# 49 instead of 32 pairs of a down projection in seven block products, and the block sums of the input kept in DRAM

## The chip, the cores and the metric

The kernel runs on one core of one Trainium2 chip. The time is device microseconds of one execution; the kernel before took 2128.32 us (median of 3 runs, 2127.16 to 2129.32). TensorE (PE) does the matrix products, VectorE (DVE) and ScalarE (ACT) the elementwise work, GpSimd (POOL) little, and the queues of SyncE (SP) and POOL issue the transfers.

## The reference

Two encoder layers over 256 tokens of width 2048: an attention sub-layer each, and then the sub-layer that the change touches, a multilayer perceptron with 8192 hidden features:

```python
D_MODEL = 2048; SEQ = 256; DEPTH = 2; D_FF = 4 * D_MODEL
for i in range(DEPTH):
    ...                                   # attention: x = x + heads @ w_out[i]
    h = rms_norm(x, norm_mlp[i])
    x = x + jnp.square(jax.nn.relu(h @ w_up[i])) @ w_down[i]
return x
```

All inputs and outputs are float32.

## The kernel before

**Exactness by splitting.** Every float32 operand of a product is split in two (`split`, L240): `hi`, a copy in the matmul's narrower type that ACT makes (L241), and `lo`, what is left, a subtraction on DVE (L242). A product of two such operands is three matmuls (hi by hi, hi by lo, lo by hi), the function `three` (L710) in the down projection.

**Weights.** A weight arrives in pieces of 128 x 1024 (512 KB), in the order of `plan`. `fetch` (L204) issues the transfer to a `raw` tile on the SP queue (L217) and splits it to `hi` and `lo`. There are four buffers each of `raw`, `hi` and `lo`; a new transfer waits until the work that read the old contents of its buffer is done, and `fetch` runs up to two pieces ahead of the piece in use (`AHEAD`).

**Up projection.** `mlp` (L680) makes 16 chunks of 512 hidden features (`chunk_out`, L318), each from 8 weight pieces, in four PSUM banks; the tags `mm` and `aux` alternate between chunks. Behind each chunk ACT and DVE add the two halves of a bank and square the positive part (L690 to L692), into a tile `ht` of [128, 4, 256]. The hidden activations stay in SBUF.

**Down projection.** It is done in two halves of 1024 output features (`half_`). In each, the 8192 hidden features are 32 pairs `j` of 2 x 128 features. A pair takes two weight pieces, and its hidden values split to `x2` (`h2_of`, L699). It is a block product of 2 x 2 blocks: two blocks of tokens (`t`), two of outputs (`n`), two of features (`kk`). An ordinary pair makes all eight block products, three matmuls each: 24 matmuls of 128 x 512.

A pair in `FAST` goes by seven block products (`seven`, L722; Winograd's form of Strassen's scheme): 21 matmuls, for sums and differences of blocks in place of the eighth product. On the weight side `fetch_sums` (L189) makes them on DVE from the pair's two raw pieces: two sums `a` (one instruction, L194, which reads both pieces), then `b` in two steps (L196, L197); `a` and `b` are split to `ah, al, bh, bl` of the tag `x2` (8 buffers). On the input side, three DVE instructions (L729, L731, L732) make block sums of the hidden values and a split makes the tile `t2` of them, tag `h2` (6 buffers, which `x2` of `h2_of` shares). Four of the seven products go to four side banks, which `add_side` adds to the result behind the last pair of `FAST`. In the second half of the first layer the tiles of the next layer's input take four of the eight `x2` buffers, and `a` and `b` are of the tag `blk` there.

**Order of the work.** The program is written with a queue of small tasks (`Task`, `tick`, `flush`) that are put between the pieces; a scheduler of the tile framework then sets the order on each engine when the program is built. On the chip each engine works through its list in that order, and waits at an instruction until what it needs is there.

Of the kernel before, what the change touches and what calls it, by code (L numbers as in the profile page):

```python
# [22 lines left out]
P = 128  # L23
# [9 lines left out]
WAIT = 2  # L33
AHEAD = 2
WARM = 16
FAST = (5, 8, 11, 14, 17, 20, 23, 26)
LAM_INIT = 0.8 - 0.6 * math.exp(-0.3 * 0)

G_ATTN, G_MEM, G_MLP = 0, 2 * KT, 4 * KT
# [8 lines left out]
def trunk(ctx: ExitStack, tc: tile.TileContext, xin, xtok, memin, pos, rel, gcol, rows,  # L48
# [12 lines left out]
    def nm(s):  # L61
        uid[0] += 1
        return f"{s}{uid[0]}"
# [4 lines left out]
    def quad(tag, shape=(P, 2, 2, 256), dt=F32R):  # L68
        return xp.tile(list(shape), dt, tag=tag, name=nm(tag), bufs={"x2": 8, "h2": 6, "blk": 10}[tag])
# [101 lines left out]
    def plan_chunks(name, chunks):  # L171
        plan.extend((name, c, j) for c in chunks for j in range(8))

    def plan_down(name):
        plan.extend((name, h, j) for h in range(2) for j in range(64))

# [27 lines left out]
    def fetch(parts=1, lead=None):  # L204

        name, c, j = plan.popleft()
        src = weights[name][c, j]
        raw = wp.tile([P, 1024], F32, tag="raw", name=nm("raw"))
        hi = wp.tile([P, 1024], F32R, tag="hi", name=nm("hi"))
        lo = wp.tile([P, 1024], F32R, tag="lo", name=nm("lo"))  # L210
        n = 1024 // parts
        seven = name.startswith("down") and j % 2 == 1 and j // 2 in FAST
        for i in range(parts):
            s = slice(i * n, (i + 1) * n)
            if lead is not None:
                lead(i)
            behind[0] = nc.sync.dma_start(raw[:, s], src[:, s])  # L217
# [22 lines left out]
    def split(hi, lo, src):  # L240
        nc.scalar.copy(hi, src)  # L241
        nc.vector.tensor_tensor(lo, src, as32(hi), op=ALU.subtract)  # L242
# [436 lines left out]

    def mlp(layer, X2, last):  # L680
        hT = []
        wide = big([P, 6, 4, S])
        for c in range(16):
            ps = chunk_out(f"up{layer}", c, 8, lambda k: X2[k], "mm" if c % 2 == 0 else "aux", 2 if c == 0 else 1)
            if c == 0:
                mlp_stats()
            ht = wide[:, c - 4] if 4 <= c < 10 else blk([P, 4, S], F32)
            for o in range(4):
                t = t1k()
                nc.scalar.copy(t, ps[o][:, 256:512])  # L690
                nc.vector.tensor_tensor(t, ps[o][:, 0:256], t, op=ALU.add)
                nc.vector.scalar_tensor_tensor(ht[:, o, :], t, 0.0, t, op0=ALU.max, op1=ALU.mult)  # L692
            hT.append(ht)
        N2 = Halves()

        def hidden(j):
            return hT[j // 2].rearrange("p k s -> p (k s)")[:, (j % 2) * 512:(j % 2) * 512 + 512]

        def h2_of(j):  # L699
            t = quad("h2", (P, 2, 512))  # L700
            split(t[:, 0, :], t[:, 1, :], hidden(j))
            return t


        for half_ in range(2):
            tag = "mm" if half_ == 0 else "aux"
            ps = [[bank(tag) for _ in range(2)] for _ in range(2)]
            chunks = (2 * half_, 2 * half_ + 1)

            def three(bank_, first_, last_, x2, xs, w2, ws):  # L710
                nc.tensor.matmul(bank_, lhsT=x2[:, 0, xs], rhs=w2[0][:, ws], start=first_, stop=False)  # L711
                nc.tensor.matmul(bank_, lhsT=x2[:, 0, xs], rhs=w2[1][:, ws], start=False, stop=False)  # L712
                nc.tensor.matmul(bank_, lhsT=x2[:, 1, xs], rhs=w2[0][:, ws], start=False, stop=last_)  # L713

            lower, upper = slice(0, 512), slice(512, 1024)

            def mms(n, t, k, two, x2):
                w2 = two[(k + n) % 2]
                three(ps[n][t], k == 0, k == 4 * KT - 1, x2, slice((k % 2) * S + t * P, (k % 2) * S + (t + 1) * P), w2,
                      upper if n else lower)  # L720

            def seven(j, two, x2):  # L722

                ah, al, bh, bl = [v.rearrange("p a n -> p (a n)") for v in sums.pop((f"down{layer}", half_, 2 * j + 1))]
                t2 = quad("h2", (P, 2, 512))
                v = t2k([P, 512])
                h = hidden(j)
                h4 = h.rearrange("p (a s) -> p a s", a=4)
                nc.vector.tensor_tensor(v[:, 0:256].rearrange("p (a s) -> p a s", a=2), h4[:, 0:4:3, :],  # L729
                                        h4[:, 1:2, :].broadcast_to([P, 2, P]), op=ALU.subtract)  # L730
                nc.vector.tensor_tensor(v[:, 256:384], h[:, 384:512], v[:, 0:128], op=ALU.add)  # L731
                nc.vector.tensor_tensor(v[:, 384:512], h[:, 256:384], v[:, 256:384], op=ALU.subtract)  # L732
                split(t2[:, 0, :], t2[:, 1, :], v)
                at = [slice(i * P, (i + 1) * P) for i in range(4)]
                f, e = j == FAST[0], j == FAST[-1]
                three(side[0], f, e, x2, at[0], two[0], lower)
                three(ps[0][0], False, False, x2, at[2], two[1], lower)
                three(ps[1][0], False, False, t2, at[3], two[0], upper)
                three(side[1], f, e, t2, at[0], (ah, al), upper)
                three(side[3], f, e, t2, at[1], (ah, al), lower)  # L740
                three(side[2], f, e, t2, at[2], (bh, bl), lower)
                three(ps[0][1], False, False, x2, at[3], (bh, bl), upper)

            def add_to(n, t, src):
                c = chunks[n]
                d = xt[:, t, c * 512:(c + 1) * 512]
                nc.vector.scalar_tensor_tensor(d, src, r2[:, t:t + 1], d, op0=ALU.mult, op1=ALU.add)
                return c, d

            def add_side():  # L750

                q1, u2, u3, u4, u5 = [t2k([P, 512]) for _ in range(5)]
                nc.scalar.copy(q1, side[0])
                nc.vector.tensor_tensor(u2, side[2], q1, op=ALU.subtract)
                nc.vector.tensor_tensor(u4, side[1], u2, op=ALU.subtract)
                nc.vector.tensor_tensor(u3, u2, side[3], op=ALU.subtract)
                nc.vector.tensor_tensor(u5, u3, side[1], op=ALU.subtract)
                add_to(0, 0, q1)
                add_to(0, 1, u4)
                add_to(1, 0, u3)  # L760
                add_to(1, 1, u5)

            def finish(n, t):
                c, d = add_to(n, t, ps[n][t])
                if last:
                    nc.sync.dma_start(out[:, t * D + c * 512:t * D + (c + 1) * 512], d)

            held = []
            for j in range(32):
                if j == FAST[0]:  # L770
# [6 lines left out]
                if j in FAST:  # L777
# [6 lines left out]
                if j == FAST[-1]:  # L784
# [12 lines left out]
        return N2  # L797

# [147 lines left out]
```

## Time and profile before

| what | us |
|---|---|
| median of 3 runs | 2128.32 |
| the profiled execution | 2127.94 |
| its span, first to last instruction | 2126.1 |
| first layer: up projection (427.8 to 785.3 of the span) | 357.5 |
| first layer: down projection, first half (785.3 to 954.0) | 168.7 |
| first layer: down projection, second half (954.0 to 1122.6) | 168.6 |
| second layer: down projection, begins at | 1784 |

The span is the time between the first and the last instruction; the execution's own time is 1.8 us longer. The granted clock of TensorE was 0.999. In the views below "busy" counts the time in which an engine worked on something, x the instructions, and a time in square brackets is how long the engine had been idle before a row, with what ended the idle time.

### The profile page before, as it was taken

What the parts mean: (1) busy time and instruction counts of PE and PEld (TensorE: products, weight loads), DVE (VectorE), ACT (ScalarE), POOL (GpSimd) and SP (SyncE); (2) the same over time, 40 slices, a digit from 0 to 9 for tenths busy, and PEclk for the clock granted to TensorE, in tenths of its full rate; (3) what the DMA queues carried; (4) which work ended last, traced back from release to release, by engine and by line L of the source; (5) the groups of instructions that cost most, each with busy time, mean ns of one, the idle gap of its engine ahead of it and who ended that gap; (6) DMA issues with size and microseconds to landing.
All of it is one profiled execution on the core that took longest, in us unless ns stands there. A gap on an engine that the chain in (4) does not pass through costs nothing.

```text
span 2126.1 us, 29324 instructions
## 1 busy us (share of the span) xinstructions
PE 2116.4 (100%) x11020; PEld 1790.6 (84%) x11020; DVE 1497.5 (70%) x2259; ACT 1130.8 (53%) x1712; POOL 34.3 (2%) x61
## 2 busy tenths in 40 slices
PE   9999999999999999999999999999999999999999
PEld 7878878888888888888888888888888888888887
DVE  7667786566565558889886677655555556888896
ACT  6456675454444446656655566554444444665564
POOL 1200020000000000000000000000000000000000
PEclk9999999999999999999999999999999999999999
DMA  8864564666666655555766556466666666566654
GB/s 292 238 211 150 159 194 154 186 180 190 191 184 196 188 190 200 197 198 198 250 205 191 178 167 187 149 180 188 188 189 190 186 192 193 190 215 210 203 193 158
DMA packets 114958, 409.23 MB, mean 192 GB/s; under 512 B 13568, under 2 KB 14336, under 8 KB 114560
## 3 DMA queue, kind: packets, MB, share of 16 engines
q1 hardware_dynamic: 111840, 401.01, 59.7%
q0 software_dynamic: 1536, 4.20, 0.8%
q10 hardware_dynamic: 1440, 2.15, 0.3%
q8 instruction: 86, 1.41, 0.3%
q14 instruction: 56, 0.46, 0.1%
HBM read 401.93 MB, written 5.37 MB: 192 GB/s over the span
## 4 chain that ended last, share of the span: by engine, by line
PE 97%; DMA 1%; DVE 1%; ACT 1%; issue 0%; SPq 0%; POOL 0%; ACTq 0%; DVEq 0%; POOLq 0%
PE mm L325 11%; PE aux L325 11%; PE mm L312 9%; PE mm L314 9%; PE mm L313 9%; PE mm L329 6%; PE aux L329 6%; PE aux L711 5%; PE aux L712 5%; PE mm L711 5%; PE mm L712 5%; PE aux L713 5%; PE mm L713 5%; PE aux L404 1%; DMA raw<-in_w_a 1%; PE aux L375 1%
## 5 line engine op out<-in xcount | busy, mean ns | idle before, releaser
L242 DVE TENSOR_TENSOR lo<-raw,hi 128x1024 fp32r<-128x1024 f32 (+1 forms) x744 | 875.4, 1190 | 535.3 <-ACT hi L241 534.0
L241 ACT CAST hi<-raw 128x1024 fp32r<-128x1024 f32 (+1 forms) x744 | 751.7, 1024 | 760.9 <-PE aux L325 193.5
L312 PE MATMUL mm<-hi,x 128*128 128x512 f32 x704 | 281.5, 401 | 0.7 <-ACT hi L241 0.7
L313 PE MATMUL mm<-lo,x 128*128 128x512 f32 x704 | 276.8, 393 | 2.6 <-DVE lo L242 2.6
L314 PE MATMUL mm<-hi,x 128*128 128x512 f32 x704 | 276.5, 393 | 0.0
L325 PE MATMUL mm<-x,hi 128*128 128x512 f32 x1024 | 247.4, 391 | 0.0
L325 PE MATMUL aux<-x,hi 128*128 128x512 f32 x1024 | 246.9, 391 | 0.0
L325 PEld LDWEIGHTS mm<-x,hi 128*128 128x128 f32 x1024 | 188.2, 188 | 36.8 <-DVE xt L675 0.5
L325 PEld LDWEIGHTS aux<-x,hi 128*128 128x128 f32 x1024 | 188.2, 188 | 36.4
L712 PE MATMUL aux<-lo,h 128*128 128x512 f32 x432 | 168.2, 389 | 0.0
L713 PE MATMUL aux<-hi,h 128*128 128x512 f32 x432 | 168.1, 389 | 0.0
L711 PE MATMUL aux<-hi,h 128*128 128x512 f32 x432 | 168.1, 389 | 0.0
L711 PE MATMUL mm<-hi,h 128*128 128x512 f32 x432 | 168.0, 389 | 0.0
L712 PE MATMUL mm<-lo,h 128*128 128x512 f32 x432 | 168.0, 389 | 0.0
L713 PE MATMUL mm<-hi,h 128*128 128x512 f32 x432 | 168.0, 389 | 0.0
L313 PEld LDWEIGHTS mm<-lo,x 128*128 128x128 f32 x704 | 133.1, 189 | 28.4 <-DVE lo L242 4.2
L314 PEld LDWEIGHTS mm<-hi,x 128*128 128x128 f32 x704 | 132.6, 188 | 28.0
L312 PEld LDWEIGHTS mm<-hi,x 128*128 128x128 f32 x704 | 132.6, 189 | 27.2 <-ACT hi L241 1.3
L329 PEld LDWEIGHTS mm<-x,lo 128*128 128x128 f32 x1024 | 131.4, 191 | 4.8
L329 PEld LDWEIGHTS aux<-x,lo 128*128 128x128 f32 x1024 | 131.3, 191 | 5.0
L329 PE MATMUL mm<-x,lo 128*128 128x256 f32 x1024 | 133.3, 283 | 0.0
L329 PE MATMUL aux<-x,lo 128*128 128x256 f32 x1024 | 132.8, 283 | 0.0
(207 smaller groups left out, 2526.0 us busy)
## 6 DMA issues: line engine op xcount, KB each, us to landing
raw<-in_w_up SPq DMA_DIRECT2D x256, 512.0 KB, 3.8
raw<-in_w_down SPq DMA_DIRECT2D x256, 512.0 KB, 4.3
raw<-in_w_a SPq DMA_DIRECT2D x72, 512.0 KB, 4.0
raw<-in_w_out SPq DMA_DIRECT2D x64, 512.0 KB, 3.6
raw<-in_w_b SPq DMA_DIRECT2D x48, 512.0 KB, 3.7
raw<-in_w_mem SPq DMA_DIRECT2D x32, 512.0 KB, 4.0
raw<-in_w_a SPq DMA_DIRECT2D x16, 256.0 KB, 5.2
blk<-bkt POOLq DMA_DIRECT2D x32, 128.0 KB, 8.6
```

The costliest lines, as they stand in the source:

```text
L241: nc.scalar.copy(hi, src)
L242: nc.vector.tensor_tensor(lo, src, as32(hi), op=ALU.subtract)
L312: nc.tensor.matmul(ps[t], lhsT=xh, rhs=hi[:, ws], start=(k == 0), stop=False)
L313: nc.tensor.matmul(ps[t], lhsT=xh, rhs=lo[:, ws], start=False, stop=False)
L314: nc.tensor.matmul(ps[t], lhsT=xl, rhs=hi[:, ws], start=False, stop=(k == KT - 1))
L325: nc.tensor.matmul(ps[o], lhsT=hi[:, cols(k % 2, o)], rhs=x2.rearrange("p a s -> p (a s)"), start=(k == 0), stop=(k == 2 * nj - 1))
L329: nc.tensor.matmul(ps[o][:, 256:512], lhsT=lo[:, cols(k % 2, o)], rhs=x2[:, 0, :], start=False, stop=False)
L375: nc.tensor.transpose(out=pt[:, h * P:(h + 1) * P], in_=qn[t][:, h * P:(h + 1) * P], identity=ident)
L404: nc.tensor.transpose(out=pt[:, kt * S + qt * P:kt * S + (qt + 1) * P], in_=p_of(qt)[:, kt * P:(kt + 1) * P], identity=ident)
L711: nc.tensor.matmul(bank_, lhsT=x2[:, 0, xs], rhs=w2[0][:, ws], start=first_, stop=False)
L712: nc.tensor.matmul(bank_, lhsT=x2[:, 0, xs], rhs=w2[1][:, ws], start=False, stop=False)
L713: nc.tensor.matmul(bank_, lhsT=x2[:, 1, xs], rhs=w2[0][:, ws], start=False, stop=last_)
```

## The change

`FAST` becomes every second pair from 3 to 27 (13 pairs instead of 8), and every second pair from 9 to 27 (`LATE`, 10 pairs) in the second half of the first layer: 13 + 10 + 13 + 13 = 49 pairs instead of 4 x 8 = 32. The block sums of the hidden values are no longer made in the down projection. A task `keep_sums` for each such pair is put behind its chunk of the up projection: the three DVE instructions, the split to a tile of tag `h2`, and a transfer of the tile (512 KB) to DRAM on the POOL queue. In the down projection `seven` reads that tile back by a transfer on the POOL queue, once in each half.

```diff
-FAST = (5, 8, 11, 14, 17, 20, 23, 26)
+FAST = tuple(range(3, 28, 2))
+LATE = tuple(range(9, 28, 2))
...
+    def fast_pairs(name, h):
+        return LATE if (name, h) == ("down0", 1) else FAST
...
-        seven = name.startswith("down") and j % 2 == 1 and j // 2 in FAST
+        seven = name.startswith("down") and j % 2 == 1 and j // 2 in fast_pairs(name, c)
...
+        def keep_sums(j):
+
+            t2 = quad("h2", (P, 2, 512))
+            v = t2k([P, 512])
+            h = hidden(j)
+            h4 = h.rearrange("p (a s) -> p a s", a=4)
+            nc.vector.tensor_tensor(v[:, 0:256].rearrange("p (a s) -> p a s", a=2), h4[:, 0:4:3, :],
+                                    h4[:, 1:2, :].broadcast_to([P, 2, P]), op=ALU.subtract)
+            nc.vector.tensor_tensor(v[:, 256:384], h[:, 384:512], v[:, 0:128], op=ALU.add)
+            nc.vector.tensor_tensor(v[:, 384:512], h[:, 256:384], v[:, 256:384], op=ALU.subtract)
+            split(t2[:, 0, :], t2[:, 1, :], v)
+            kept[j] = dp.tile([P, 2, 512], F32R, name=nm("kept"))
+            nc.gpsimd.dma_start(kept[j], t2)
...
             hT.append(ht)
+            for j in (2 * c, 2 * c + 1):
+                if any(j in fast_pairs(f"down{layer}", h) for h in range(2)):
+                    Task([lambda j=j: keep_sums(j)], wait=2)
...
+        flush()
...
             def seven(j, two, x2):
...
-                v = t2k([P, 512])
-                h = hidden(j)
-                h4 = h.rearrange("p (a s) -> p a s", a=4)
-                nc.vector.tensor_tensor(v[:, 0:256].rearrange("p (a s) -> p a s", a=2), h4[:, 0:4:3, :],
-                                        h4[:, 1:2, :].broadcast_to([P, 2, P]), op=ALU.subtract)
-                nc.vector.tensor_tensor(v[:, 256:384], h[:, 384:512], v[:, 0:128], op=ALU.add)
-                nc.vector.tensor_tensor(v[:, 384:512], h[:, 256:384], v[:, 256:384], op=ALU.subtract)
-                split(t2[:, 0, :], t2[:, 1, :], v)
+                nc.gpsimd.dma_start(t2, kept[j])
```

The other lines of the diff put `fast[0]` and `fast[-1]` where `FAST[0]` and `FAST[-1]` stood.

The scheduler's order on DVE in the middle of the first layer's first half, before: one ordinary pair, one ordinary pair, and a pair by seven products. `lo` are splits of weight pieces, `h2` splits of hidden values (from `t2k`: of the block sums), L194 makes the sums `a`, L196 and L197 the two steps of `b`, and `x2` are the splits of `a` and `b`.

```order
L242 TENSOR_TENSOR lo1605_8438<-raw1603_8436,hi1604_8437 128x1024
L242 TENSOR_TENSOR lo1608_8444<-raw1606_8442,hi1607_8443 128x1024
L242 TENSOR_TENSOR h21638_8582<-big930_4604,h21638_8582 128x512
L242 TENSOR_TENSOR h21651_8634<-big930_4604,h21651_8634 128x512
L194 TENSOR_TENSOR x21616_8485<-raw1610_8475,raw1613_8481 128x1024
L196 TENSOR_TENSOR x21617_8486<-x21616_8485,raw1610_8475 128x512
L197 TENSOR_TENSOR x21617_8486<-x21617_8486,raw1613_8481 128x512
L242 TENSOR_TENSOR x21619_8493<-x21616_8485,x21618_8492 128x1024
L242 TENSOR_TENSOR x21621_8495<-x21617_8486,x21620_8494 128x1024
L242 TENSOR_TENSOR lo1612_8477<-raw1610_8475,hi1611_8476 128x1024
L242 TENSOR_TENSOR lo1615_8483<-raw1613_8481,hi1614_8482 128x512
L242 TENSOR_TENSOR h21658_8673<-blk1288_6773,h21658_8673 128x512
```

The same engine at the same place, with the change: first an ordinary pair (raw1574 and raw1577) and the pair by seven products behind it (raw1582 and raw1585). Lines have moved: L246 is the split, L198 makes `a`, L200 and L201 make `b`.

```order
L246 TENSOR_TENSOR lo1576_8212<-raw1574_8210,hi1575_8211 128x1024
L246 TENSOR_TENSOR lo1579_8218<-raw1577_8216,hi1578_8217 128x1024
L198 TENSOR_TENSOR x21588_8258<-raw1582_8248,raw1585_8254 128x1024
L246 TENSOR_TENSOR lo1584_8250<-raw1582_8248,hi1583_8249 128x1024
L200 TENSOR_TENSOR x21589_8259<-x21588_8258,raw1582_8248 128x512
L246 TENSOR_TENSOR lo1587_8256<-raw1585_8254,hi1586_8255 128x512
L201 TENSOR_TENSOR x21589_8259<-x21589_8259,raw1585_8254 128x512
L246 TENSOR_TENSOR x21591_8266<-x21588_8258,x21590_8265 128x1024
L246 TENSOR_TENSOR h21615_8363<-big930_4604,h21615_8363 128x512
L246 TENSOR_TENSOR x21593_8268<-x21589_8259,x21592_8267 128x1024
L246 TENSOR_TENSOR h21622_8402<-big930_4604,h21622_8402 128x512
```

And right behind it the next ordinary pair (raw1595 and raw1598) and the next pair by seven products (raw1603 and raw1606):

```order
L198 TENSOR_TENSOR x21609_8348<-raw1603_8338,raw1606_8344 128x1024
L246 TENSOR_TENSOR lo1597_8302<-raw1595_8300,hi1596_8301 128x1024
L246 TENSOR_TENSOR lo1600_8308<-raw1598_8306,hi1599_8307 128x1024
L246 TENSOR_TENSOR lo1605_8340<-raw1603_8338,hi1604_8339 128x1024
L200 TENSOR_TENSOR x21610_8349<-x21609_8348,raw1603_8338 128x512
L246 TENSOR_TENSOR lo1608_8346<-raw1606_8344,hi1607_8345 128x512
L201 TENSOR_TENSOR x21610_8349<-x21610_8349,raw1606_8344 128x512
L246 TENSOR_TENSOR x21612_8356<-x21609_8348,x21611_8355 128x1024
L246 TENSOR_TENSOR h21636_8453<-big930_4604,h21636_8453 128x512
L246 TENSOR_TENSOR x21614_8358<-x21610_8349,x21613_8357 128x1024
L246 TENSOR_TENSOR h21643_8492<-big930_4604,h21643_8492 128x512
```

Before, `a` stood behind the splits of both ordinary pairs that precede its pair. Now it stands behind the splits of the one ordinary pair in every second case, and ahead of them in the others: the two forms alternate, six times the second form in each half with 13 such pairs, twice in the half with 10.

On DVE in the up projection, behind the work of a chunk (L713 and L714 were L691 and L692), the block sums (L697, L699, L700) and their split stand between the splits of the next chunk's weights:

```order
L714 SCALAR_TENSOR_TENSOR blk1351_7060<-t1k1354_7069 128x256
L714 SCALAR_TENSOR_TENSOR blk1351_7060<-t1k1355_7073 128x256
L246 TENSOR_TENSOR lo1365_7089<-raw1363_7087,hi1364_7088 128x1024
L697 TENSOR_TENSOR t2k1367_7126<-blk1351_7060 128x256
L246 TENSOR_TENSOR lo1371_7136<-raw1369_7134,hi1370_7135 128x1024
L699 TENSOR_TENSOR t2k1367_7126<-blk1351_7060,t2k1367_7126 128x128
L700 TENSOR_TENSOR t2k1367_7126<-blk1351_7060,t2k1367_7126 128x128
L246 TENSOR_TENSOR lo1374_7142<-raw1372_7140,hi1373_7141 128x1024
L246 TENSOR_TENSOR h21366_7125<-t2k1367_7126,h21366_7125 128x512
L246 TENSOR_TENSOR lo1377_7180<-raw1375_7178,hi1376_7179 128x1024
```

Before, at the other chunks' ends the same place held only the splits of weights, apart from a few block sums of early pairs that the scheduler had put there already.

More of the change, by code (lines that the diff above doesn't have):

```diff
@@ L681, in mlp, with hidden @@
         hT = []
+        kept = {}
         wide = big([P, 6, 4, S])
+        def hidden(j):
+            return hT[j // 2].rearrange("p k s -> p (k s)")[:, (j % 2) * 512:(j % 2) * 512 + 512]
+        def keep_sums(j):
[10 more added lines that the diff above has]
+            nc.gpsimd.dma_start(kept[j], t2)
         for c in range(16):
@@ L693, in mlp @@
             hT.append(ht)
+            for j in (2 * c, 2 * c + 1):
+                if any(j in fast_pairs(f"down{layer}", h) for h in range(2)):
+                    Task([lambda j=j: keep_sums(j)], wait=2)
         N2 = Halves()
-        def hidden(j):
-            return hT[j // 2].rearrange("p k s -> p (k s)")[:, (j % 2) * 512:(j % 2) * 512 + 512]
         def h2_of(j):
@@ L708, in mlp @@
             chunks = (2 * half_, 2 * half_ + 1)
+            fast = fast_pairs(f"down{layer}", half_)
             def three(bank_, first_, last_, x2, xs, w2, ws):
@@ L725, in seven @@
                 t2 = quad("h2", (P, 2, 512))
[L726 to L733 removed]
+                nc.gpsimd.dma_start(t2, kept[j])
                 at = [slice(i * P, (i + 1) * P) for i in range(4)]
[L735 removed]
+                f, e = j == fast[0], j == fast[-1]
                 three(side[0], f, e, x2, at[0], two[0], lower)
@@ L769, in mlp @@
             for j in range(32):
-                if j == FAST[0]:
+                if j == fast[0]:
                     side = [bank("aux" if half_ == 0 else "mm") for _ in range(4)]
@@ L776, in mlp @@
                     continue
-                if j in FAST:
+                if j in fast:
                     seven(j, two, x2)
@@ L783, in mlp @@
                                 mms(n, t, 2 * j + kk, two, x2)
-                if j == FAST[-1]:
+                if j == fast[-1]:
                     add_side()
```

## The prediction

> **What bounds the kernel now.** I read the page first: busy time by engine, and the chain of work that ended last.
>
> ```profile
> span 2126.1 us, 29324 instructions
> PE 2116.4 (100%) x11020; PEld 1790.6 (84%) x11020; DVE 1497.5 (70%) x2259; ACT 1130.8 (53%) x1712; POOL 34.3 (2%) x61
> PE 97%; DMA 1%; DVE 1%; ACT 1%; issue 0%; SPq 0%; POOL 0%; ACTq 0%; DVEq 0%; POOLq 0%
> ```
>
> PE is on 97% of the chain. But a busy PE can be a slow PE, so I took the rate next, from the timeline of PE in a down projection, nine matmuls apart (818.20 to 819.79 stand between):
>
> ```profile
> 817.97 0.39 PE L711 MATMUL mm<-hi,h 128*128 128x512 f32 x1
> ...
> 820.01 0.39 PE L711 MATMUL mm<-hi,h 128*128 128x512 f32 x1
> ```
>
> One starts every 2.04 / 9 = 0.2267 us. An ordinary pair is 24 x 0.2267 = 5.44 us, one by seven products 21 x 0.2267 = 4.76 us. A half of the first layer's down projection has 24 of the one and 8 of the other: 168.6 us. The windows by stage (the first row is the up projection, the others the two halves) show just that, so PE doesn't stall there at all:
>
> ```profile
> core 0: us, PE busy (x) PEld busy (x) DVE busy (x) ACT busy (x) POOL busy (x), PEclk, DMA share, GB/s
> 427.80:785.30 357.50, 357.50 (x2058) 315.84 (x2057) 206.73 (x282) 158.05 (x204) 0.00 (x0) 1.00 0.61 189
> 785.30:954.00 168.70, 168.70 (x746) 139.71 (x745) 143.45 (x168) 99.05 (x125) 0.00 (x0) 1.00 0.58 198
> 954.00:1122.60 168.60, 168.60 (x754) 139.82 (x752) 146.79 (x182) 100.76 (x130) 3.50 (x2) 1.00 0.63 215
> ```
>
> DVE is busy 85% of the first half (143.45 of 168.70): the engine to watch when work moves from PE to DVE. The clock is 1.00 and cancels.
>
> **What the change takes away.** 17 more pairs by seven products, three matmuls less each: 51 x 0.2267 = 11.56 us of PE's time, if PE stays the bound.
>
> **What DVE has to do for it.** The timeline of DVE in the first half, one pair by seven products and the ordinary pair behind it:
>
> ```profile
> 850.05 1.29 DVE L242 TENSOR_TENSOR h<-big,h 128x512 fp32r<-128x512 f32 x2
> 851.34 1.23 DVE L194 TENSOR_TENSOR x<-raw,raw 128x1024 f32<-128x1024 f32 x1
> 852.60 0.69 DVE L196 TENSOR_TENSOR x<-x,raw 128x512 f32<-128x512 f32 x1
> 853.32 0.69 DVE L197 TENSOR_TENSOR x<-x,raw 128x512 f32<-128x512 f32 x1
> 853.93 2.42 DVE L242 TENSOR_TENSOR x<-x,x 128x1024 fp32r<-128x1024 f32 x2
> 856.27 1.82 DVE L242 TENSOR_TENSOR lo<-raw,hi 128x1024 fp32r<-128x1024 f32 x2
> 858.01 0.69 DVE L242 TENSOR_TENSOR h<-big,h 128x512 fp32r<-128x512 f32 x1
> 860.10 2.36 DVE L242 TENSOR_TENSOR lo<-raw,hi 128x1024 fp32r<-128x1024 f32 x2 [1.41 <-ACT hi L241]
> 862.38 0.69 DVE L242 TENSOR_TENSOR h<-t2k,h 128x512 fp32r<-128x512 f32 x1
> ```
>
> Ends overlap the next start, so I count from start to start: two splits of 1024 take 862.38 - 860.10 = 2.28, 1.14 each; the pair at 856.27 (one of 1024, one of 512) takes 1.74, so 0.60 for 512. A pair by seven products without its block sums is `a`, one `lo` and two splits of sums (4 x 1.14), the two steps of `b`, the short `lo` and one hidden split (4 x 0.60): 6.96 us. An ordinary pair is 2 x 1.14 + 0.60 = 2.88. With the change the two alternate: DVE needs 9.84 us where PE needs 5.44 + 4.76 = 10.20. It fits with 0.36 to spare. The block sums would not have fitted:
>
> ```profile
> L729 DVE TENSOR_TENSOR t2k<-big 128x256 f32<-128x256 f32 x16 | 6.6, 421 | 0.0
> L731 DVE TENSOR_TENSOR t2k<-big,t2k 128x128 f32<-128x128 f32 x16 | 4.4, 286 | 0.0
> L732 DVE TENSOR_TENSOR t2k<-big,t2k 128x128 f32<-128x128 f32 x16 | 4.5, 289 | 0.3
> ```
>
> These and a split of 512 take about 1.4 us, overlaps taken off: 11.2 a round.
>
> **Where the sums go.** 26 of them (13 a layer) stand in the up projections, 1.4 us of DVE and a cast of 0.6 on ACT each. DVE is busy there 206.73 of 357.50 us, and the timeline behind a chunk shows that a delay of that size is already borne: two hidden splits between the weights' splits, and then it waits for ACT, which waits for PE.
>
> ```profile
> 457.55 0.69 DVE L242 TENSOR_TENSOR h<-blk,h 128x512 fp32r<-128x512 f32 x1
> 458.23 1.23 DVE L242 TENSOR_TENSOR lo<-raw,hi 128x1024 fp32r<-128x1024 f32 x1
> 461.98 1.23 DVE L242 TENSOR_TENSOR lo<-raw,hi 128x1024 fp32r<-128x1024 f32 x1 [2.53 <-ACT hi L241]
> ```
>
> I cost them at nothing, hidden by PE's 22 us a chunk. If that cover were gone, 26 x 1.4 = 36 us. The stores and loads on POOL's queue block nobody behind them: POOL has no other work there but two selects on the bias table, and tag `h2` has six buffers of which a round takes three, so each load may start when PE is done with the pair four back, 15 us before its tile is needed.
>
> **The loop that I expect to bind.** The 0.36 us of spare time counts only while DVE never waits. A weight's transfer waits for its buffer, by SP's waits in the first half:
>
> ```profile
> SPq L217 <- DVE lo L242: 140.6, 63, 8.2
> ```
>
> With four `raw` buffers and two pairs of two pieces in turn, the pieces of one pair by seven products always take the buffers of the one before. The last reader of its second piece is the second step of `b`. So from there to the next `a` lies at least a transfer, D:
>
> ```profile
> raw<-in_w_down SPq DMA_DIRECT2D x256, 512.0 KB, 4.3
> L217 SPq DMA_DIRECT2D raw<-in_w_down x4: 327/328/328, 845.7 to 850.2; - x4
> DMA to landing us min/median/max: 3.7/4.4/4.5
> ...
> L217 SPq DMA_DIRECT2D raw<-in_w_down x4: 327/328/328, 1064.4 to 1067.8; - x4
> DMA to landing us min/median/max: 3.8/5.1/5.9
> ```
>
> Issued four in 4.5 us, the slowest takes 4.5 us; four in 3.4 us, 5.9. Where `a` stands behind the ordinary pair's splits, DVE has 3.48 (two splits of sums, two hidden) + 2.28 = 5.76 us of other work in the meantime. Where the scheduler put `a` ahead of them (every second time), it has 3.48 only, and stands still with those two splits, ready to go, queued behind `a`; PE waits for them.
>
> Worked out, with times from PE's start of a pair by seven products: the ordinary pair's casts on ACT need `hi` buffers that PE frees 0.68 us before and at that start, 2.00 us for both,
>
> ```profile
> 859.01 2.00 ACT L241 CAST hi<-raw 128x1024 fp32r<-128x1024 f32 x2 [1.93 <-issue]
> ```
>
> so its second `lo` ends at 2.8, and `a`, `lo`, step, short `lo`, step end at 2.8 + 1.14 + 1.14 + 0.60 + 0.60 + 0.69 = 7.0. In the next round `a` starts at 7.0 + D, and the second `lo` ends 3.51 later: at D + 0.31 after that round's start (10.20). PE reads it 4.76 + 4 x 0.2267 = 5.67 after it. From then on two rounds take DVE D + 6.45 (`a` to the last step) + 9.84 = D + 16.29 against PE's 20.40: it falls D - 4.11 further behind each time.
>
> D lies between 4.5 and 5.9; one below 4.2 would make the loop harmless. The changed kernel moves five 512 KB transfers in 10.2 us where four went in at the same pace before, so I take the middle, 5.2. Then it falls behind 1.09 a time: second `lo` at 5.51, 6.60, and so on; PE stalls 0 at the first, 0.93 at the second, 1.09 at each of four more: 5.3 us a half, for three halves 15.9. The half with ten such pairs has the bad order twice, 0.9, and the bias table's transfer falls in it:
>
> ```profile
> big<-bsv SPq DMA_DIRECT2D x1, 3072.0 KB, 12.2
> raw<-in_w_down SPq DMA_DIRECT2D x5, 512.0 KB, 6.3
> ```
>
> Weights beside it take 6.3 us; between nothing and 3 us, I take 1.5. Stalls together: 18.3.
>
> **The sum.** 2127.94 (the profiled execution) - 11.56 + 18.3 = 2134.7; the median of the runs is 0.4 above that execution: **2135**. With D = 4.5 a half stalls 1.1 us, together 3.3: 2120. With D = 5.9 a half stalls 9.5, together 33.8 with 5.3 in the half with ten: 2151. The break-even lies at D = 4.87.
>
> A rule of the Trainium skill speaks against the change. DMA: Bandwidth & Descriptors fits a transfer as 2.0 us plus bytes at 436 GB/s (Anatomy of one DMA), 3.2 us for 512 KB, and says that an engine takes turns between POOL's and SP's queues (SWDGE vs HWDGE vs iDMA). The trace comes near it for one alone (3.7 the fastest of four) and agrees for two behind each other (4.4). Were the reloaded sums always in the way as a third, as in rival 2, D would be an estimated 5.6, and the sum 2143.
>
> **The rivals.** (1) *Not slower: the loop stays under PE.* The reload starts about 4.8 us after a round's start and may be through before the critical piece is issued at 7 to 8; then D is as in the calmer row, 4.5: 2120, and with no stall at all 2116.8. For it: SP's pieces are 1.2 us apart in the loop, as at 845.7. Against: four outstanding are more than the usual one or two. It decides below D = 4.87. (2) *The transfers collide*: reload, both pieces and the ordinary pair's at once, D = 5.9: 2151. For it the row at 1064.4; against, only a quarter more bytes a second. (3) *The up projections pay.* If the split behind the sums came late at each chunk, up to 36 us: 2153. Against: 2.53 us of idle time behind each of those rows. (4) *The change doesn't do what it says*: the order shows the 51 matmuls gone and the sums moved, so only a cost of nothing on both sides, 2128, is left; hardly.
>
> **How the numbers follow.** A measurement of this kernel can't tell less than 0.2%, 4.3 us, from no change. Chances: the forecast (D 4.87 to 5.5) 0.42, rival 1 0.36, rival 2 0.16, rival 3 0.04, rival 4 0.02. Range 2118 to 2150, which leaves out no stall at all and the worst collision; the forecast's own is 2128 to 2141. Faster by over 0.2% needs D below 4.65: most of rival 1, 0.30. Within 0.2% (2124.1 to 2132.6, D 4.65 to 5.1): 0.18. Slower: 0.52.
>
> **What would show it.** PE with 10969 matmuls, and idle before L736 with `lo` (L246) as releaser, 12 to 20 us in all, in the ordinary pairs of the down projections, from the fourth pair by seven products on; `a` (L198) waiting for `raw` some 1 to 2 us every second time, D between 4.8 and 5.5; the up projections at 357.5 as before. If PE has no such idle time, the loop was wrong; if DVE is full without waiting for transfers, my durations were; if the up projections grow, rival 3.

## The result and the profile after

The changed kernel takes **2152.32 us** (median of four runs, 2150.59 to 2153.23), the kernel before 2128.26 (four runs, 2127.16 to 2129.32) beside it: a ratio of 1.0114, 95% interval [1.0099, 1.0128]. It is slower, as forecast, but by 24 us where the prediction had 7, and lies above its range of 2118 to 2150. The profiled execution took 2150.59.

The page of the changed kernel: span, busy time of TensorE and VectorE, the chain of work that ended last, and the transfers of the down weights and of the reloaded sums.

```profile
span 2148.8 us, 29639 instructions
PE 2121.0 (99%) x10969; PEld 1780.1 (83%) x10969; DVE 1548.5 (72%) x2320; ACT 1160.9 (54%) x1740; POOL 73.7 (3%) x136
PE 76%; DVE 12%; DMA 8%; issue 3%; ACT 1%; DVEq 0%; SPq 0%; ACTq 0%
raw<-in_w_down SPq DMA_DIRECT2D x256, 512.0 KB, 4.7
h<-kept POOLq DMA_DIRECT2D x49, 512.0 KB, 4.8
```

The busy share of PE hardly says anything (99% for 100%). The chain says more: PE's part of it fell from 97% to 76%, and VectorE and DMA, 1% each before, have 12% and 8%. The weights' transfers take 4.7 us in the median, 4.3 before.

The windows by stage of the changed kernel (first the up projection, then the four halves of the down projections) and of the kernel before (its last three halves; the first is in the prediction, 168.70). The columns are the prediction's: length, then busy time of PE, PEld, DVE, ACT and POOL, granted clock, DMA share, GB/s.

```profile
425.70:783.20 357.50, 357.50 (x2058) 315.81 (x2057) 219.76 (x315) 164.93 (x216) 7.53 (x14) 1.00 0.67 209
...
783.20:956.60 173.40, 168.69 (x730) 135.84 (x729) 155.13 (x180) 104.50 (x128) 6.37 (x12) 1.00 0.67 229
956.60:1137.80 181.20, 175.42 (x756) 142.76 (x755) 142.77 (x162) 100.70 (x129) 8.32 (x12) 0.97 0.69 233
1798.10:1971.40 173.30, 168.78 (x731) 135.92 (x730) 154.63 (x179) 103.29 (x125) 6.89 (x13) 1.00 0.68 232
1971.40:2144.90 173.50, 169.00 (x730) 135.60 (x729) 149.62 (x168) 99.76 (x117) 6.36 (x12) 1.00 0.66 226
```

```profile
954.00:1124.40 170.40, 170.40 (x761) 141.32 (x760) 148.59 (x184) 101.80 (x133) 3.50 (x2) 1.00 0.63 216
1784.60:1953.35 168.75, 168.75 (x746) 139.73 (x745) 147.65 (x186) 98.46 (x124) 0.00 (x0) 1.00 0.60 199
1953.35:2122.20 168.85, 168.85 (x745) 139.34 (x743) 137.83 (x156) 93.50 (x114) 0.00 (x0) 1.00 0.58 194
```

The up projection is as long as before to the hundredth, 357.50, with VectorE 13 us busier in it. A half with thirteen pairs by seven products needs 729 x 0.2267 = 165.3 us, and takes 8.1, 8.0 and 8.2 us more. The half with ten needs 738 x 0.2267 = 167.3 and takes 13.9 more; before, the same half had 1.7 over its 744 matmuls (work and no stall: 16 small transposes for the next layer, from 959.4 and 965.8 on). So 24.3 us are lost in three halves and 12.2 in the fourth: 36.5, less the 11.56 saved, is the 25 us between the two spans' down projections. (The profiled execution reached the up projections 2.1 us earlier than the one of before; that is the start of the program.)

**The loop, on VectorE.** Its timeline through one `a` (L198) that stands behind the ordinary pair's splits and the next, which stands ahead of them; behind it SyncE's issues of the two pieces in between, and their landing:

```profile
2010.95 2.35 DVE L246 TENSOR_TENSOR lo<-raw,hi 128x1024 fp32r<-128x1024 f32 x2
2013.22 1.22 DVE L198 TENSOR_TENSOR x<-raw,raw 128x1024 f32<-128x1024 f32 x1
...
2016.70 0.69 DVE L201 TENSOR_TENSOR x<-x,raw 128x512 f32<-128x512 f32 x1
...
2020.17 0.69 DVE L246 TENSOR_TENSOR h<-big,h 128x512 fp32r<-128x512 f32 x1
2022.78 1.23 DVE L198 TENSOR_TENSOR x<-raw,raw 128x1024 f32<-128x1024 f32 x1 [1.92 <-DMA raw<-in_w_down]
2023.92 3.49 DVE L246 TENSOR_TENSOR lo<-raw,hi 128x1024 fp32r<-128x1024 f32 x3
```

```profile
L221 SPq DMA_DIRECT2D raw<-in_w_down x2: 328/328/328, 2016.2 to 2017.5; - x2
...
DMA to landing us min/median/max: 5.2/5.2/5.2
```

The second step of `b` ends at 2017.39, the piece is issued at once and takes 5.2 us; VectorE runs out of work at 2020.86 and stands for 1.92 us, with three `lo` behind `a` in its queue. From `b` to `a` it is 5.39 us: the D of the prediction. Over the twenty places where `a` waited so (worked out from the same rows), D goes from 4.42 to 5.84, median 5.40. (At four of them the view names PE as the releaser, but there too the piece had landed 0.12 us before.)

**The same moment on TensorE**, and the last such stall of that half:

```profile
2024.30 0.39 PE L735 MATMUL aux<-hi,h 128*128 128x512 f32 x1
2025.20 0.50 PE L736 MATMUL aux<-lo,h 128*128 128x512 f32 x1 [0.51 <-DVE lo L246]
2025.54 0.40 PE L737 MATMUL aux<-hi,h 128*128 128x512 f32 x1
2025.78 0.40 PE L735 MATMUL aux<-hi,h 128*128 128x512 f32 x1
2026.33 0.50 PE L736 MATMUL aux<-lo,h 128*128 128x512 f32 x1 [0.16 <-DVE lo L246]
2026.67 0.39 PE L737 MATMUL aux<-hi,h 128*128 128x512 f32 x1
...
2111.28 0.39 PE L735 MATMUL aux<-hi,h 128*128 128x512 f32 x1
2112.39 0.50 PE L736 MATMUL aux<-lo,h 128*128 128x512 f32 x1 [0.72 <-DVE lo L246]
```

The two stalls are four times two rounds apart: (2111.28 - 2024.30) / 4 = 21.75 us, against D + 16.29 = 21.69 by the prediction's formula, and 20.40 that TensorE needs. The start-to-start times give the loss at one place: 0.90, 0.34 and 0.55, 0.34 where 0.23 is due, 1.22 us in all. The idle column shows 0.51 + 0.16 of it, since it counts from the modelled end of a matmul (0.39) and a matmul is due after 0.2267. So the groups by line understate the loss:

```profile
L736 PE MATMUL aux<-lo,h 128*128 128x512 f32 x400 | 159.3, 399 | 6.0 <-DVE lo L246 5.9
L736 PE MATMUL mm<-lo,h 128*128 128x512 f32 x379 | 150.2, 396 | 9.2 <-DVE lo L246 9.1
```

15.0 us by this view; by the lengths of the stages more than twice that.

**The half with ten pairs.** SyncE's issue of the bias table (L618, 3 MB, at 1051.9) and of the four weights behind it, TensorE where they came late, and the windows before and after that place:

```profile
L618 SPq DMA_DIRECT2D big<-bsv x1: 326/326/326, 1051.9 to 1051.9; - x1
...
DMA to landing us min/median/max: 12.9/12.9/12.9
```

```profile
L221 SPq DMA_DIRECT2D raw<-in_w_down x4: 327/328/328, 1053.0 to 1058.2; - x4
...
DMA to landing us min/median/max: 12.0/12.8/13.7
```

```profile
1067.71 0.95 PE L735 MATMUL aux<-hi,h 128*128 128x512 f32 x2 [2.47 <-ACT hi L245]
1069.18 0.79 PE L736 MATMUL aux<-lo,h 128*128 128x512 f32 x1 [0.52 <-DVE lo L246]
1069.78 0.63 PE L737 MATMUL aux<-hi,h 128*128 128x512 f32 x1
1070.20 0.63 PE L736 MATMUL aux<-lo,h 128*128 128x512 f32 x1
```

```profile
1061.00:1068.00 7.00, 4.53 (x20) 3.48 (x19) 1.55 (x4) 1.53 (x3) 3.00 (x2) 1.00 0.93 367
1068.00:1075.00 7.00, 6.48 (x16) 4.57 (x16) 7.00 (x8) 3.84 (x5) 0.56 (x2) 0.51 0.69 241
```

All four weights took about the table's own time, 12 to 13.7 us. VectorE and ScalarE stood still for most of the 7 us from 1061 on (busy 1.55 and 1.53), TensorE for 2.47. Then the granted clock fell to 0.51 for 7 us, and the matmuls ran 0.42 us apart. The place costs 6.4 us (the sum of the start-to-start times over 0.2267 from 1064.9 to 1074.9), and VectorE, which has 0.36 us to spare in a round, is still late at the half's end, where the sums of the side banks are added: another 3.7 us at 1119 to 1126.

### The profile page after: what moved, and what is told of

The parts are those of the page before. It is cut to its first block, busy times and chain, and to the rows that moved or that the text cites. A ratio compares the mean times of both kernels' runs of the same rounds, so it can differ in the third digit from the quotient of the medians.

```text
span 2148.8 us, 29639 instructions
## 1 busy us (share of the span) xinstructions
PE 2121.0 (99%) x10969; PEld 1780.1 (83%) x10969; DVE 1548.5 (72%) x2320; ACT 1160.9 (54%) x1740; POOL 73.7 (3%) x136
## 4 chain that ended last, share of the span: by engine, by line
PE 76%; DVE 12%; DMA 8%; issue 3%; ACT 1%; DVEq 0%; SPq 0%; ACTq 0%
PE mm L329 11%; PE aux L329 11%; PE mm L316 9%; PE mm L317 9%; PE mm L318 9%; DMA raw<-in_w_down 7%; DVE lo L246 6%; PE aux L333 6%; PE mm L333 6%; PE aux L737 2%; PE aux L736 2%; PE aux L735 2%; PE mm L736 2%; PE mm L737 2%; PE mm L735 2%
## 5 line engine op out<-in xcount | busy, mean ns | idle before, releaser
L246 DVE TENSOR_TENSOR lo<-raw,hi 128x1024 fp32r<-128x1024 f32 (+1 forms) x744 | 867.6, 1177 | 477.8 <-ACT hi L245 475.7
L736 PE MATMUL aux<-lo,h 128*128 128x512 f32 x400 | 159.3, 399 | 6.0 <-DVE lo L246 5.9
L735 PE MATMUL aux<-hi,h 128*128 128x512 f32 x400 | 157.0, 395 | 2.5 <-ACT hi L245 2.5
L736 PE MATMUL mm<-lo,h 128*128 128x512 f32 x379 | 150.2, 396 | 9.2 <-DVE lo L246 9.1
L737 PE MATMUL aux<-hi,h 128*128 128x512 f32 x400 | 156.8, 394 | 1.8 <-DVE h L246 1.8
L737 PE MATMUL mm<-hi,h 128*128 128x512 f32 x379 | 147.7, 390 | 0.0
L735 PE MATMUL mm<-hi,h 128*128 128x512 f32 x379 | 147.6, 389 | 0.0
L245 ACT CAST x<-x 128x1024 fp32r<-128x1024 f32 x78 | 82.0, 1052 | 113.1 <-DVE x L201 101.3
```

## The experiments

Each time is a median, beside runs of the kernel before on the same chip (2127.4 to 2127.7); ratios are to it.

**1. The order.** `a` is put behind the split of the ordinary pair's second piece on its engine; the order of the down projections' splits is then the calm one in every round.

```diff
-        nc.vector.tensor_tensor(a, first.rearrange("p (a n) -> p a n", a=2),
+        with tc.issue_after(newest[-2].ins): nc.vector.tensor_tensor(a, first.rearrange("p (a n) -> p a n", a=2),
...
-                split(hi[:, s], lo[:, s], raw[:, s])
+                newest.append(split(hi[:, s], lo[:, s], raw[:, s]))
...
-        nc.vector.tensor_tensor(lo, src, as32(hi), op=ALU.subtract)
+        return nc.vector.tensor_tensor(lo, src, as32(hi), op=ALU.subtract)
```

> The changed kernel, with `a` (L198) always put behind the ordinary pair's two `lo` splits on VectorE; no instruction is added or taken away. Loop theory (VectorE stands at `a` for a transfer while the ordinary pair's splits queue behind it, six times in each of three halves, 8.0 + 7.8 + 7.8 us of stalls, and 1.8 in the fourth): the transfer of 4.4 to 5.8 us then lies beside 5.76 us of other work, the stalls go, 2126 to 2131 us, with the half whose bias table is loaded as long as before. Rival (VectorE simply has too much work a round, the waits only show it): the same work in another order, 2149 to 2155 us.

Measured: **2120.47 us** (2119.24 to 2123.07, seven runs), ratio 0.9966 [0.9954, 0.9977]: 32 us less than the changed kernel, with the same instructions, and better than expected: the half with the bias table gained too. VectorE's timeline in it, two rounds:

```profile
1035.26 2.35 DVE L246 TENSOR_TENSOR lo<-raw,hi 128x1024 fp32r<-128x1024 f32 x2
1037.53 1.23 DVE L198 TENSOR_TENSOR blk<-raw,raw 128x1024 f32<-128x1024 f32 x1
...
1045.10 2.35 DVE L246 TENSOR_TENSOR lo<-raw,hi 128x1024 fp32r<-128x1024 f32 x2
1047.37 1.22 DVE L198 TENSOR_TENSOR blk<-raw,raw 128x1024 f32<-128x1024 f32 x1
```

A round of VectorE without a wait takes 1047.37 - 1037.53 = 9.84 us, the prediction's figure to the hundredth. Its rival "too much work for VectorE" falls. `a` still waits for transfers, but less, and nothing that TensorE needs stands behind it (changed kernel first, then this one):

```profile
  DMA raw<-in_w_down: 34.3, 22
  PE aux L737: 8.0, 4
```

```profile
  DMA raw<-in_w_down: 13.0, 19
```

The second layer's down projection has 0.2 us over 1458 x 0.2267; the first still has 6.3 us, of which 1.6 are the transposes of before and 4.5 stalls in the half with the table (12.1 in the changed kernel). The table is as near to the weights here as there: the first was issued 1.1 us behind it, and four landed after 11.4 to 13.0 us.

**2. The reloads.** The second operand of the three products on the hidden sums is the pair's own split, so the reload falls away; the sums are still made and stored. VectorE's order in the loop, with the bad rounds, stays.

```diff
-                t2 = quad("h2", (P, 2, 512))
-                nc.gpsimd.dma_start(t2, kept[j])
+                t2 = x2
```

> The changed kernel without the 49 reloads (the second operand of three of the seven products is the hidden pair's own split instead of its block sums, so these products are not the reference's); the sums are still made and stored. Theory that the reload stretches the transfers of the weights: from the second step of `b` to `a` falls from 5.4 to between 4.5 and 5.0 us, a stall of two rounds by as much: 2134 to 2143 us. Rival (the pieces stand in each other's way only, the reload has its own room): still 5.2 to 5.8 us, 2149 to 2153 us.

Measured: 2126.29 us (2124.3 to 2128.99, ten runs), ratio 0.9997 [0.9987, 1.0006]: below both expectations. The step of `b` and the `a` of one bad round:

```profile
2019.59 0.68 DVE L201 TENSOR_TENSOR x<-x,raw 128x512 f32<-128x512 f32 x1
2025.11 1.23 DVE L198 TENSOR_TENSOR x<-raw,raw 128x1024 f32<-128x1024 f32 x1 [1.37 <-DMA raw<-in_w_down]
```

D is 4.84 here and 4.73 in the median of twenty (4.25 to 5.93), 0.67 less than with the reloads, as the first theory had it. For three halves the gain is the prediction's own formula, which the expectation had not used to its end: with D = 4.73 the second `lo` comes at 5.04 and falls 0.62 behind each time, so it is late only from the third time on (0.6 and then 0.62 three times, some 2.5 us a half; the trace has 2.3, 3.9 and 2.6 us of stalls in them, where the changed kernel had 24.3 in all). The reloads moved D from just below the break-even of 4.87 to well above. Most of the rest of the 26 us lies in the half with ten pairs, which has 2.7 us of stalls instead of 12.1: here the first weight was issued 4.8 us after the bias table, and not 1.1. So this run shows what the reload does to D, but not that all 26 us are D's.

**3. A fifth raw buffer**, paid for with smaller pools (raw 5 for 4; t1k 3 for 4; sm 8 for 36).

> The changed kernel with five raw buffers for four, paid for with two smaller pools elsewhere (t1k 3 for 4, sm 8 for 36). Loop theory: the second piece of a pair by seven products no longer takes the buffer whose last reader is the step just before, so its transfer starts a round's share earlier; the waits of `a` go, and the down projections lose 20 us or more: 2126 to 2133 us, unless the smaller pools cost time in the attention, which the windows by stage would show. Rival (the transfers are limited by what the queues move, not by when the buffer comes free): `a` still waits for raw, 2145 us or more.

Measured: 2185.1 us (2181.12 to 2187.94), ratio 1.0271 [1.0254, 1.0287]: 33 us *slower* than the changed kernel, and against the loop theory's hope. The rival's figure holds (`a` still waits, 2145 us or more), but not its reason, as experiment 4 shows. VectorE's timeline in it:

```profile
875.74 1.23 DVE L198 TENSOR_TENSOR x<-raw,raw 128x1024 f32<-128x1024 f32 x1 [2.75 <-DMA raw<-in_w_down]
877.07 0.69 DVE L200 TENSOR_TENSOR x<-x,raw 128x512 f32<-128x512 f32 x1
877.68 2.35 DVE L246 TENSOR_TENSOR lo<-raw,hi 128x1024 fp32r<-128x1024 f32 x2
```

With the free buffer the scheduler puts `a` (and the first step of `b`) ahead of the ordinary pair's splits in nearly *every* round (all but two at the start of the last half and three in the half with ten): the chance of the loop to catch up in the other rounds is gone.

**4. The fifth buffer with the order of experiment 1.**

> Five raw buffers as in e_raw5, with the order edit of e_order. In e_raw5 `a` stood ahead of the ordinary pair's splits in every round instead of every second one, and it ran 2185 us. Theory that this order made it slow: with `a` behind them it is as fast as e_order, 2117 to 2122 us. Rival (the smaller pools or more transfers at once made it slow): 2150 us or more.

Measured: 2120.06 us (2118.76 to 2120.84), ratio 0.9962 [0.9947, 0.9977], the same as experiment 1 and 65 us below experiment 3. So the order alone made that one slow, neither the pools nor the transfers; and once the order is right the buffers don't matter.

**5. The bias table in six pieces**, each behind a fetch of the next layer's first projections, its masks as a last stage and the heads that read it behind that.

```diff
+            with tc.issue_after(behind[0].ins):
+                nc.sync.dma_start(flat[:, 1024 * i:1024 * i + 1024], bsv[:, 1024 * i:1024 * i + 1024])
...
+        return Task([lambda i=i: part(i) for i in range(6)] + [masks], wait=1, gap=1)
```

> The changed kernel with the bias table loaded in six pieces behind the weights of the next layer's first projections instead of in one piece in the first layer's second down half. Theory that this transfer makes the two stalls of that half (6.4 us near 1065 and 3.7 near 1120, slow matmuls behind them included): both go, 2141 to 2144 us. Rival (VectorE falls behind there with ten pairs by seven products, the table or not): 2149 to 2153 us, with stalls at the half's end still.

Measured: 2147.5 us (2146.38 to 2148.34), ratio 1.0095 [1.008, 1.011]: 4.8 less, half of what was expected. Both stalls of the half are gone (its largest waits are now 1.5, 0.7 and 1.0 us, at 1047, 1069 and 1091), but these are three stalls of the loop's kind: in the place of the table's wait the half goes on with the bad rounds, and loses 5.2 us instead of 12.1. The first half of that layer loses 11.0 us instead of 8.0, mainly since one of its loop stalls was followed by a stretch of half clock (the last section shows it). The run alone can't part the table and the loop; the next one does.

**6. Order and table together.**

> The order edit of e_order and the bias table in six pieces of e_bias together. In e_order the first layer's down projection kept 6.3 us of stalls, 1.6 of them the two at a half's end that stand before the change too; the rest is in the half with the bias table. Theory that the table's one transfer makes them: another 4 to 5 us go, 2115 to 2117 us. Rival (the table costs as much wherever it is loaded, or the ten pairs fall behind without it): 2119 to 2122 us.

Measured: **2117.00 us** (2114.91 to 2118.03), ratio 0.9947 [0.9932, 0.9962], 35 us below the changed kernel and the fastest of all: close to the time that the prediction gave for no stall at all, 2116.8 (2116.1, if worked out from the 2127.7 beside this run). By stage its first down projection has 1.8 us over its matmuls, 1.6 of them the transposes of before, and the second 0.2. With the order mended the table still cost 3.5 us, where in the changed kernel the half with it lost 12. A fifth buffer on top of it:

> e_both with the five raw buffers (and smaller pools) of e_raw5o. e_both has no stalls left in the down projections beyond the 0.8 + 0.8 us that stand in the kernel before too, so by the loop theory a fifth buffer has nothing to take away: 2115 to 2119 us. Rival (the transfers still cost something that no gap shows): 2113 us or less.

Measured: 2119.39 us (2118.15 to 2119.8), no gain, as the loop theory says.

**7. Block sums in the down projections again**, for 49 pairs, with the order of experiment 1: the table of pairs without the move to DRAM.

> The order edit of e_order, with the block sums made in the down projections as before the change (nothing stored or reloaded), for 49 pairs. Theory that VectorE is full there: a round takes it 9.84 + 1.4 = 11.2 us where TensorE needs 10.2, 1.0 us for each of some 46 rounds above e_order: 2155 to 2175 us. Rival (VectorE has room, the reload costs as much as it saves): 2117 to 2125 us.

Measured: 2146.52 us (2144.55 to 2149.16), ratio 1.0088 [1.0073, 1.0103]. VectorE is full, as the prediction said (in the first half, 786 to 956, it is busy 162.0 of 170.0 us, and the window's row shows it):

```profile
786.00:956.00 170.00, 164.47 (x706) 133.53 (x705) 162.00 (x204) 106.45 (x135) 0.00 (x0) 0.98 0.59 191
```

but the time is 26 us above experiment 1 and not 46: the first stall of a half comes only at 886, 100 us into it, which fits a lead of VectorE that is used up first (the expectation had left it out; no run tells it apart). So, with this order, moving the sums is worth 26 us to 49 pairs.

**8. The move alone**, for the 32 pairs of before (FAST as before, LATE the same).

> The move alone: the pairs by seven products of the kernel before (32), with their block sums made in the up projections, stored and reloaded. Theory that the move costs nothing where VectorE has 15% to spare: 2125 to 2130 us, no stall at `lo` beyond those of before. Rival (the stores in the up projections or the reloads stall TensorE by themselves): 2133 us or more.

Measured: 2134.88 us (2131.25 to 2139.11, seven runs), ratio 1.0037 [1.0025, 1.0048]. The move costs 7 us by itself, and scatters. A second profile:

> e_move once more, for a second profile: its seven runs went from 2131 to 2139 us, and the one profiled was the fastest; it had 2.1 us of new stalls, near 1094 in the half with the bias table. Theory that what varies is that half (how long the transfers behind the table take): a slower run has its excess there, at 1040 to 1130 us. Rival (each of the 32 reloads costs a little): the excess lies in all four halves.

It took 2134.57 us, with 5.6 us over its matmuls in the first layer's down projection (1.6 of them the transposes) and 4.6 in the second's, where the profile of 2131 had 4.6 and 0.3. The excess isn't tied to the half with the table, but it doesn't lie in all four halves either: 3.4 and 4.4 us are in the second half of each layer, 0.4 and none in the first halves. Neither expectation is met. With the order edit and the table in pieces:

> e_move with the order edit and the bias table in six pieces. Theory that the move's cost lies in the half with the table and nowhere else: 2125 to 2129 us. Rival (the stores and reloads cost something wherever they stand): 2132 us or more, as e_move.

Measured: 2137.51 us (2132.65 to 2139.54), ratio 1.0045 [1.003, 1.006]: no better, and with stalls in all four halves (2.5, 2.5, 0.9 and 5.1 us), as the rival has it. SyncE's four issues ahead of one stall of 1.8 us on TensorE (at 2064.4), with a reload issued on POOL's queue at 2049.07 among them:

```profile
L221 SPq DMA_DIRECT2D raw<-in_w_down x4: 327/328/328, 2049.0 to 2052.5; - x4
...
DMA to landing us min/median/max: 3.8/6.8/7.2
```

And without the reloads (the sums still made and stored; VectorE's order differs a little, since the reloads' buffers are free, but `a` stands where it did):

> e_move without its 32 reloads (the second operand is the hidden pair's own split, as in e_noload); the sums are still made and stored, and VectorE still has no block sums in the down projections. Theory that the reloads alone make the move cost time (they stretch the weights' transfers beside them to 6.6 to 7.2 us): 2125 to 2129 us, no new stalls. Rival (something else in the move, the stores or the changed order, costs it): 2132 us or more.

Measured: 2127.89 us (2126.41 to 2128.39, ten runs), ratio 1.0001 [0.9991, 1.0011]; weights land in 4.3 us in the median as before (4.6 with reloads), and no stall is left in the down projections. The sums in the up projections and their stores cost nothing; the reloads cost the 7 us. Why 32 of them cost 7 us here, and the 49 of experiment 6 nothing that its stages show, stays open.

## Why the prediction was right, and where it failed

| term, us | predicted | measured |
| --- | --- | --- |
| 51 matmuls fewer | 11.56 | 51 by the page (11020 and 10969); 10.7 us in experiment 6 |
| sums in the up projections | 0 | 0 (357.50 and 357.50; experiment 8 without reloads) |
| stalls, three halves with thirteen pairs | 15.9 | 24.3 |
| stalls, half with ten and the bias table | 2.4 | 12.2 |

The step that failed is the size of the stalls: 18.3 us in the sum, 36.5 measured. 8.4 us of the difference are in the loop of three halves, 9.8 in the half with the bias table.

- **The mechanism was right.** TensorE's rate, VectorE's 9.84 us a round, the loop over the raw buffers, the two orders of `a`, `lo` as the releaser, and D + 16.29 us for two rounds all came out within 0.1 us, and changing nothing but the order took away every stall of the three halves with thirteen pairs. The second layer, which has no bias table, shows it alone: six stalls a half, one in every second round.
- **D was mis-sized**: "I take the middle, 5.2" came out as 5.40. That adds 0.2 us to each stall. The rival that carried D = 5.9 got the time nearly right (2151), but not by its own way: D was 5.4, and a third of the loss had another cause. The prediction's other estimate, 5.6, missed by as much on the other side; the fit of the Trainium skill that it used (DMA: Bandwidth & Descriptors, Anatomy of one DMA) is stated for transfers that GpSimd issues, and the weights are SyncE's.
- **The loop does not start from rest.** The prediction let it begin with VectorE on time, "0 at the first, 0.93 at the second". The first stall was as long as the others (0.71 + 0.11 + 0.33 + 0.11 us from 814.5 on): already the good round ahead of it waited 1.04 us for a piece that took 5.9 us. With six full stalls of 21.75 - 20.40 = 1.35 us a half loses 8.1, which is what was measured. D and this start are the 8.4 us between the two columns for the three halves; by the formula, as an estimate, 3.6 for D = 5.40 and 4.8 for the start.
- **The bias table was mis-sized most**: "between nothing and 3 us, I take 1.5". The row it came from, weights landing in 6.3 us beside the table, was of a kernel that issued its next weight 6.1 us after the table (at 1043.8, the table at 1037.7). Here the first weight went out 1.1 us after it, three more and a reload within 6.3 us, and all landed only after the table had, 12 to 13.7 us after their issue; VectorE had little spare time to make good for it, and the clock fell. About 10 of the half's 12.2 us (6.4 + 3.7) are this, and experiments 5 and 6 took both stalls away. But it is the table together with the bad order: in experiment 1 the table and its weights were as slow, and the half lost 4.5 us.
- **The reloads "block nobody behind them"** was true of POOL's queue and missed the point: they are paid for in other queues' transfers. As an estimate inside D (the middle of two bounds) they were counted, but as a term of their own they were not; measured, they add 0.67 us to D in the loop, and 7 us to a kernel that has no such loop. Rival 1, the loop staying under TensorE, is nearly what happens without them (experiment 2: D = 4.73, 2126), though 8.8 us of stalls are left in three halves.
- **The sign to look for was in the wrong view.** "Idle before L736, 12 to 20 us" was met (15.0) while the loss was 36: that column counts from a modelled end.
- Rival 3 (the up projections pay) and rival 4 (nothing happens) fell.

## What to carry to other kernels

On an engine that works strictly in order, an instruction that waits for a transfer must stand behind everything that is ready and wanted elsewhere: here the same instructions take 2152 or 2120 us by the place of one of them, and a further buffer made it worse, because the scheduler used it to put that instruction still earlier. A transfer on a queue of its own is not free where a loop waits for transfers (0.67 us in the median here): price it by what it adds to the slowest of those beside it, and look for the break-even. And take a stall's size from start-to-start times or from the length of the stage, not from the idle column of a pipelined engine.

## What the runs showed of the hardware that was not expected

A short idle time of TensorE can halve its clock, and where it falls counts. In the traces' clock records the stretches of half clock, away from the program's ends, are 3.41 or 6.83 us long, at 0.50, and within a run their starts lie whole multiples of 3.413 us apart (in the changed kernel 1068.06 and 1122.67, 16 of them). Count TensorE's idle time in steps of this grid: in the two steps ahead of these starts it is 2.47 and 1.83 us. In experiment 5 a loop stall did the same, with 3.41 - 1.76 = 1.65 us idle in one step. In experiment 3 a matmul came 2.85 us late at 937 and the clock stayed: the gap lies across two steps, 1.59 us in one and 1.27 in the next. The step of experiment 5 and the one behind it, and the two of experiment 3:

```profile
837.19:840.60 3.41, 1.76 (x7) 0.97 (x6) 3.41 (x4) 1.68 (x3) 0.54 (x1) 1.00 0.50 126
840.60:844.01 3.41, 3.41 (x9) 2.67 (x8) 3.41 (x6) 1.02 (x1) 0.00 (x0) 0.50 0.97 342
```

```profile
935.24:938.65 3.41, 1.82 (x9) 1.16 (x7) 2.70 (x4) 1.53 (x2) 0.00 (x0) 1.00 0.07 24
938.65:942.06 3.41, 2.14 (x8) 1.49 (x9) 3.41 (x4) 3.41 (x6) 0.00 (x0) 1.00 0.24 88
```

Over all traces, start and end of the program left out, half clock followed each of the four steps with over 1.8 us of idle time, three of the ten with 1.5 to 1.75, and none with less. The loop's stalls in the changed kernel had at most 1.13 us in a step, and there the clock stayed at 1.00.

The Trainium skill (TensorE: Matmul & The Clock Gate, Part 1: The HAM clock gate) describes a gate that looks at activity in free-running windows of some 3.4 us and drops to half rate; the 3.413 us and the 0.50 agree. Its rule (same page, HAM oscillation), no idle gaps above 3.4 us, is too generous by these rows.

Also, at full clock every wait of TensorE for a split in the changed kernel's down projections cost 0.11 us more than the wait: the matmul that waited is followed after 0.33 to 0.34 us instead of 0.23.
